# A hybrid SSD / RWKV-7 layer with a ConvGLU on one core: other plans for the recurrence phase, steps cut in two, and the SSD step sizes half a chunk sooner

## The chip, the core and the metric

The kernel runs on one core of a Trainium2 chip. The metric is the device time of one execution in microseconds (us); the time of a kernel is the median of its runs. The engines are named as the profile names them: PE (TensorE, matmuls; PEld its weight loads), DVE (VectorE), ACT (ScalarE), POOL (GpSimd) and SP (SyncE, which issues nearly all DMAs, in order). Each engine works its instructions off in program order.

## What is computed

The reference, cut to its skeleton (one layer, 2048 tokens, width 1024):

```python
xn = _rms_norm(h, pre_mix_norm[l])
proj = (xn @ w_in[l]).astype(jnp.float32)
p_ssd, p_rwkv = jnp.split(proj, [SSD_COLS], axis=-1)
y_ssd = _ssd_mixer(p_ssd, ...)      # conv, softplus step sizes, chunks of 128, gate, norm
y_rwkv = _rwkv7_mixer(p_rwkv, ...)  # token shift, low-rank decay and gates, 8 heads of 64
mix = jnp.concatenate([y_ssd, y_rwkv], axis=-1).astype(h.dtype) @ w_out[l]
h = h + _rms_norm(mix, post_mix_norm[l])
hn = _rms_norm(h, pre_ffn_norm[l])
u = _causal_dwconv(hn @ ffn_w_up[l], ffn_conv_w[l], ffn_conv_b[l])
gate, val = jnp.split(u, 2, axis=-1)
f = (jax.nn.silu(gate) * val) @ ffn_w_down[l]
h = h + _rms_norm(f, post_ffn_norm[l])
```

The RWKV-7 mixer is a recurrence over tokens, `S = S * w + sa * b + v * k` with `sa = S a`. The kernel computes it in chunks of 64 tokens, for which a triangular system per head and chunk has to be solved.

## The kernel before

Three phases follow one another, each a Python generator that emits instructions.

**Recurrence phase** (`phase_R`): 16 blocks of 128 tokens. A block normalises and transposes its tokens (`load`), multiplies them with 14 column groups of `w_in` (steps `d.0` to `d.13`, two per PSUM bank, 24 matmuls each) and with 8 groups for the SSD convolution (`conv.0` to `conv.7`, 24 matmuls each, followed by six tap instructions per pair of groups on DVE and two on POOL). From the `d` results come the decay (`low_rank`: tanh, two small matrix products `zw` and `za` in 16 matmuls, a running sum), the keys (`keys`, `norm`, `receptance`), the Gram matrices (`gram`, chunks 0 and 1) and the triangular solve: `solve` writes blocks of the Gram matrix to DRAM (`ATd`), reads them back laid out one system per partition (`atl`), runs 31 steps of two small tensor instructions each (`tmp`, then `xl`; 62 instructions, each needing the one before), and sends the result through DRAM (`XTd`) into `XT`. The block before (`b`) uses its `XT`: `own`, `merge` (`XW` on DVE, `pw` and `po` on PE), `update`, `state`, `gate`, and `finish` (group norm, transposes `yt`, output).

What is emitted in which order is a written plan: one string per kind of iteration (`FIRST`, `SECOND`, `PLAN` for blocks 2 to 14, `LAST`, and `DRAIN`, in which `S` runs a step of the SSD phase). `f` is the block of this iteration, `b` the block before, `n` the next one. PE runs exactly the order of the plan. On the other engines a scheduler orders the instructions and keeps dependencies; each of them is in order at run time too, so an instruction that waits holds everything behind it on its engine.

**SSD phase** (`phase_S`): 16 chunks of 128 tokens, in pairs. `steps` computes the step sizes of a pair (32 short matmuls `dt` and some 20 instructions of 128x16 on DVE, up to `da`), `sums` the running sums (matmul `acs`), `flip` and `rows` bring them into rows; then decay, state, output projection (`o`), `post` (norm, residual, transposes `ht`). `S_PLAN` is the order within a chunk; `s.` steps run in even chunks, `t.` steps in odd ones, both for the next pair.

**Feed-forward phase** (`phase_F`): up and down products of the ConvGLU, a seven-product scheme on halves.

The lines that matter below: L193 and L197 (`load`), L206 (the matmuls of `d` and `conv`), L384, L388, L389, L394 (`low_rank`: the low part of the operand `WX`, the two kinds of matmul, the running sum), L367 (taps), L443 and L447 (Gram and its masked copy `G`), L459, L463, L477, L483 (the DMAs of `solve`), L471 and L474 (its steps), L515 (`XW`), L522 (`pw`), L611 to L617 (`finish` up to `yt`), L790 and L795 (`da`, `acs`), L978 and L983 (`xi`, `ht`).

## Time and profile before

| | us |
|---|---|
| three runs | 2787.14, 2790.0, 2790.8; median 2790.0 |
| the profiled execution | 2795.42, of which its span is 2793.4 |
| recurrence phase with its drain | 0 to about 1069 (last `yt`) |
| SSD phase | to about 1470 |
| feed-forward phase | the rest |

In the stretch from 140 to 960 us, blocks 2 to 14 and a little more, PE is busy for 745.7 of 820 us, DVE for 617.4, ACT for 422.8 and POOL for 336.2, and the mean granted TensorE clock is 0.96. From 1130 to 1400 us, in the SSD phase, PE is busy for 244.5 of 270 us.

How to read the rows that follow: a row of the timeline has the start, the duration, the engine, the line, the operation, the tiles, the count, and in brackets how long the engine sat idle before it and what ended that. A row of the waits has the waiting instruction, what released it, the total in us, the number of times and the longest. A row of the windows has the busy time (with the number of instructions) of PE, PEld, DVE, ACT and POOL, then the granted clock of TensorE, the share of the DMA engines and GB/s. The chain of waits is followed back from the last instruction; "issue" in it is time for which the profile shows no wait. Matmul groups with "xN" are N matmuls in a row.

### The profile page before, as it was taken

The page shows a single profiled execution, that of the slowest core. Times are in us where ns is not written, and L with a number is a line of the kernel's source. Part 1 is how long each engine was busy: PE and PEld are TensorE (multiplying, and loading weights), DVE is VectorE, ACT ScalarE, POOL GpSimd, SP SyncE. Part 2 cuts the span into 40 slices and gives each one's busy share as a digit, 9 for nine tenths or more (in the row PEclk, how much of TensorE's full clock was granted, in tenths as well). Part 3 has the DMA queues.
Part 4 walks back from the last instruction along what each step waited for, and adds up shares of the span by engine and source line. Part 5 has one row for each costly group of instructions (what it writes and reads, how often), then busy time and mean ns, then how long its engine had stood idle before and what let it go on. Part 6 is the DMA issues. An engine that isn't in the chain of part 4 may idle for free.

```text
span 2793.4 us, 54157 instructions
## 1 busy us (share of the span) xinstructions
PE 2533.3 (91%) x21458; PEld 1595.1 (57%) x21468; DVE 1942.4 (70%) x3711; ACT 1196.6 (43%) x2448; POOL 1237.7 (44%) x1286
## 2 busy tenths in 40 slices
PE   5898899999989989899898798989988899999998
PEld 5888888888878865455443343434433344444443
DVE  7778767777777766556767858787879744554557
ACT  5455555445555534344444444434344333132132
POOL 5234434434434423333457855657476532132234
PEclk8999999999999989999999899999999999999999
DMA  6212121221211144333355334343434633333243
GB/s 213 52 43 60 47 48 45 52 51 43 60 47 45 40 149 137 107 105 124 136 183 190 126 138 155 136 154 132 151 129 155 226 99 106 102 101 102 86 137 126
DMA packets 261278, 302.62 MB, mean 108 GB/s; under 512 B 133664, under 2 KB 168864, under 8 KB 257696
## 3 DMA queue, kind: packets, MB, share of 16 engines
q1 hardware_dynamic: 259440, 296.54, 33.4%
q8 instruction: 168, 2.75, 0.4%
q10 hardware_dynamic: 1584, 2.63, 0.3%
q14 instruction: 86, 0.70, 0.1%
HBM read 188.11 MB, written 110.99 MB: 107 GB/s over the span
## 4 chain that ended last, share of the span: by engine, by line
PE 42%; DVE 25%; POOL 11%; DMA 8%; issue 8%; ACT 4%; SPq 2%; POOLq 0%; DVEq 0%; ACTq 0%
PE u L1182 16%; PE d L1329 10%; PE d L206 4%; DVE ca L367 3%; PE o L958 3%; DVE xl L474 3%; DVE tmp L471 3%; POOL fa L1087 2%; DMA HN<-hT 2%; DMA atl<-ATd 2%; DVE a L1219 2%; POOL us L1083 1%; PE l L1410 1%; POOL p L1247 1%; DMA ATd<-G 1%
## 5 line engine op out<-in xcount | busy, mean ns | idle before, releaser
L1182 PE MATMUL u<-b,w 128*128 128x512 f16 x3696 | 820.4, 384 | 52.1 <-DVE C L1191 36.5
L1182 PEld LDWEIGHTS <-w 128*128 128x128 f16 x3696 | 365.3, 99 | 503.5 <-issue 80.5
L206 PE MATMUL d<-xt,wr 128*128 128x129 f16 x5376 | 356.3, 230 | 7.2 <-DVE xt L197 5.1
L206 PEld LDWEIGHTS <-wr 128*128 128x128 f16 x5376 | 346.0, 103 | 28.9 <-issue 23.0
L1329 PE MATMUL d<-dw,fa 128*128 128x512 f16 x1512 | 339.8, 384 | 18.3 <-DVE dw L159 17.6
L1329 PEld LDWEIGHTS <-fa 128*128 128x128 f16 x1596 | 158.1, 99 | 222.7 <-issue 34.7
L1191 DVE TENSOR_TENSOR C<-u,C 128x512 f32<-128x512 f32 x220 | 150.6, 685 | 188.6 <-PE u L1182 151.4
L206 PE MATMUL c<-xt,wc 128*128 128x131 f16 x3072 | 201.2, 223 | 0.3 <-ACT tr L344 0.3
L206 PEld LDWEIGHTS <-wc 128*128 128x128 f16 x3072 | 184.7, 98 | 5.8 <-issue 0.7
L367 DVE SCALAR_TENSOR_TENSOR ca<-rc,cw,ca 128x128 f32<-128x128 f32 x384 | 156.5, 440 | 39.9 <-POOL ca L362 38.3
L1338 DVE TENSOR_TENSOR acc<-d,acc 128x512 f32<-128x512 f32 x212 | 139.8, 682 | 57.3 <-PE d L1329 56.6
L1219 DVE SCALAR_TENSOR_TENSOR p<-C,fpar,p 128x1024 f32<-128x1024 f32 x88 | 121.8, 1384 | 70.2 <-ACT p L1217 70.1
L159 DVE SCALAR_TENSOR_TENSOR w<-us,w 128x512 f16<-128x512 f32 x132 | 121.4, 925 | 68.2 <-ACT w L158 67.1
L471 DVE TENSOR_TENSOR tmp<-atl,xl 128x60 f32<-128x60 f32 (+24 forms) x496 | 122.1, 246 | 52.2 <-DMA atl<-ATd 41.9
L1086 ACT ACTIVATE fa<-p 128x512 f16<-128x512 f32 x132 | 79.6, 624 | 177.4 <-DVE p L1223 94.1
L1087 POOL TENSOR_TENSOR fa<-p,fa 128x512 f16<-128x512 f32 x120 | 151.5, 1273 | 3.6 <-ACT fa L1086 3.6
L474 DVE TENSOR_TENSOR xl<-xl,tmp 128x60 f32<-128x60 f32 (+24 forms) x496 | 137.4, 277 | 11.8
L158 ACT ACTIVATE w<-us 128x512 f16<-128x512 f32 x132 | 80.5, 623 | 139.3 <-POOL us L1083 99.9
L1219 DVE SCALAR_TENSOR_TENSOR a<-C,fpar,a 128x1024 f32<-128x1024 f32 x88 | 128.9, 1465 | 4.5 <-ACT a L1217 1.7
L362 POOL TENSOR_SCALAR ca<-rc,cw,cb 128x128 f32<-128x128 f32 x128 | 69.7, 553 | 135.4 <-ACT rc L359 61.7
L1216 POOL COPY C<-fcarry 128x2 f32<-128x2 f32 x88 | 40.9, 467 | 158.4 <-ACT a L1217 77.3
L1221 POOL COPY fcarry<-C 128x2 f32<-128x2 f32 x88 | 34.4, 391 | 169.1 <-DVE C L1191 168.7
(318 smaller groups left out, 4583.9 us busy)
## 6 DMA issues: line engine op xcount, KB each, us to landing
UW<-w SPq DMA_DIRECT2D x154, 256.0 KB
w<-UW SPq DMA_DIRECT2D x154, 256.0 KB
us<-in_w_u_dram SPq DMA_DIRECT2D x44, 512.0 KB
DW<-dw SPq DMA_DIRECT2D x70, 256.0 KB
dw<-DW SPq DMA_DIRECT2D x56, 256.0 KB
hs<-HN SPq DMA_DIRECT2D x48, 256.0 KB
r<-in_w_d_dram SPq DMA_DIRECT2D x10, 1024.0 KB
xin<-in_x_dram SPq DMA_DIRECT2D x16, 512.0 KB
```

Of the source, the lines that this page charges most:

```text
L159: eng.scalar_tensor_tensor(out=lo, in0=src, scalar=scale, in1=hi, op0=ALU.mult, op1=ALU.subtract)
L206: nc.tensor.matmul(ps, w[:, a, kt, :], xt[:, kt, b, cols], start=n == 0, stop=n == 3 * KT - 1)
L367: V.scalar_tensor_tensor(out=acc[:, q], in0=raw[:, q, k:k + 128], scalar=cw[:, g + q, k:k + 1], in1=acc[:, q], op0=ALU.mult, op1=ALU.add)
L471: V.tensor_tensor(out=tmp[:, :m, :n], in0=atl[:, j, j + 1:32].unsqueeze(1).to_broadcast([P, m, n]), in1=xl[:, :m, j:j + 1].to_broadcast([P ...
L474: V.tensor_tensor(out=xl[:, :m, j + 1:32], in0=xl[:, :m, j + 1:32], in1=tmp[:, :m, :n], op=ALU.add)
L958: nc.tensor.matmul(self.po, l, WO[:, v, (kt + 4) % KT, ds_], start=k == 0, stop=k == 23)
L1087: eng.tensor_tensor(out=lo, in0=src, in1=hi, op=ALU.subtract)
L1182: nc.tensor.matmul(bk[at], self.w[i][:, u, k, :], self.half.b[i][:, k, v, :], start=start and n == 0, stop=n == 11, skip_group_check=True)
L1191: V.tensor_tensor(out=o, in0=ps, in1=a, op=ALU.add)
L1219: V.scalar_tensor_tensor(out=a, in0=c[:, 2 - d:1026 - d], scalar=cw[:, g, 2 - d:3 - d], in1=a, op0=ALU.mult, op1=ALU.add)
L1329: nc.tensor.matmul(ps, pairs[m].a[i][:, u, t * P:t * P + P], ws[n][m][:, v, :], start=new and m == 0 and u == v == 0, stop=m == N - 1 and ...
L1338: V.tensor_tensor(out=acc[j][:, t], in0=ps, in1=acc[j][:, t], op=ALU.add)
```

## The change

Every plan of the recurrence phase is rewritten; of the tables a line or two is shown, and what they do to the engines further down. `low_rank` becomes `low.0` (tanh and operand split) and `low.1` (matmuls and running sum), `finish` becomes `finish.0` (the statistics, at the end of an iteration) and `finish.1` (transposes and output, emitted in the iteration after, as `a.finish.1`), `load` becomes `load.0` and `load.1` with work between them.

```diff
 S_PLAN = """
-c.begin c.decay.0 Z c.off p.norm c.keys Z c.decay.1 p.o.0.0 Z t.sums p.o.0.1 t.flip Z n.rows q.post.0 c.y c.state
-p.o.1.0 q.post.1 p.o.1.1 s.steps
+c.begin c.decay.0 Z c.off p.norm c.keys Z c.decay.1 p.o.0.0 Z t.sums s.steps p.o.0.1 t.flip Z n.rows q.post.0 c.y c.state
+p.o.1.0 q.post.1 p.o.1.1
...
 PLAN = """
-f.d.0 f.d.1 b.values f.d.2 f.d.3 f.low_rank f.d.4 f.d.5 f.keys f.d.6 ...
+f.d.0 f.d.1 f.d.2 a.finish.1 b.values f.d.3 f.low.0 f.d.4 f.d.5 f.low.1 f.d.6 f.d.7 f.d.8 f.keys f.d.9 f.conv.0
...
-            def low_rank(self):
+            def low(self, part):
+                sides = [(slice(64 * i, 64 * i + 64), slice(64 - 64 * i, 128 - 64 * i)) for i in range(2)]
+                if part == 0:
+                    X = self.X = wk.tile([P, 2, P], F16, name="WX" + self.sf, tag="WX")
+                    S.activation(WA[0:64], WA[0:64], AF.Tanh)
+                    for i, (own, far) in enumerate(sides):
+                        S.activation(X[own, i], WA[own], AF.Copy)
+                        V.tensor_tensor(out=X[far, i], in0=WA[own], in1=X[own, i], op=ALU.subtract)
+                    S.activation(GL, GL, AF.Tanh, scale=0.5)
+                    V.tensor_scalar(out=GL, in0=GL, scalar1=0.5, scalar2=0.5, op0=ALU.mult, op1=ALU.add)
+                    return
...
                     for j in range(4):
                         js = slice(j * P, (j + 1) * P)
-                        nc.tensor.matmul(ps[:, j, :], wl[:, i, js], X[:, i], start=True, stop=False)
-                        nc.tensor.matmul(ps[:, j, :], wl[own, 2, js], X[own, i], start=False, stop=True)
+                        nc.tensor.matmul(
+                            ps[:, j, :], wl[:, i, js], X[:, i], start=j == 0, stop=False, skip_group_check=True)
+                    for j in range(4):
+                        js = slice(j * P, (j + 1) * P)
+                        nc.tensor.matmul(
+                            ps[:, j, :], wl[own, 2, js], X[own, i], start=False, stop=j == 3, skip_group_check=True)
...
-                cum = self.tl("cum", tag="kkn")
+                cum = Pv
...
                 for q in range(4):
-                    nc.sync.dma_start(
+                    K.marks["atl"] = nc.sync.dma_start(
...
+                chain = G_ if it == iters - 1 else V
                 for j in range(31):
                     n, m = 31 - j, j // 4 + 1
-                    V.tensor_tensor(
+                    chain.tensor_tensor(
...
-            nc.sync.dma_start(st, w_z[g])
+            pace(tc, K, nc.sync.dma_start(st, w_z[g]), "atl")
...
-            nc.sync.dma_start(self.xt, XN[self.b])
+            pace(tc, K, nc.sync.dma_start(self.xt, XN[self.b]), "atl")
...
-            nc.sync.dma_start(self.xbc, XC[self.b])
+            pace(tc, K, nc.sync.dma_start(self.xbc, XC[self.b]), "atl")
```

So: the running sum is written where `Pv` will stand and no longer into the buffer of `kkn`; the 62 solve instructions of the last block go to POOL instead of DVE; and the first loads of the SSD phase stand behind the `atl` reads on SP's queue (`pace` adds an order to the queue, no wait). Lines of the changed kernel are shifted by up to 22.

**The matmuls of the low-rank step on PE**, in block 6. Before, these rows follow the last matmul of `d.3` and go on alternating, a matmul of 128 rows (L388) and one of 64 (L389), eight times for `zw` and `za` together:

```order
L206 MATMUL d_2_7707<-xt_7455,wr 128x129
L388 LDWEIGHTS wl
L388 MATMUL zw_7768<-WX_7765,wl 128x128
L389 LDWEIGHTS wl
L389 MATMUL zw_7768<-WX_7765,wl 128x128
```

Now they follow the last matmul of `d.5`; this is the place, after four matmuls of 128 rows (L404), where the four of 64 rows (L408) begin:

```order
L404 LDWEIGHTS wl
L404 MATMUL zw_6753<-WX_6690,wl 128x128
L408 LDWEIGHTS wl
L408 MATMUL zw_6753<-WX_6690,wl 128x128
L408 LDWEIGHTS wl
```

The step has moved 48 matmuls (`d.4` and `d.5`) back, `yt`, `vt` and `bo` now stand between `d.2` and `d.3`, and the two shapes change four times in a block instead of sixteen.

**DVE, from the arrival of `XT` to the Gram matrix**, in block 6. Before, from the transposes `XW` to the last masked copy `G` of the first chunk (`kkn`, `AR`, `BK` are the normalised keys and the Gram operands, `tr` and `tk` receptance and key, `ca` taps):

```order
L515 STREAM_TRANSPOSE XW_7011<-XT_232 32x256 x2
L415 SCALAR_TENSOR_TENSOR kkn_6565<-sq_6564,kkn_6565 128x512
L346 SCALAR_TENSOR_TENSOR tr_6563<-raw_8_6936,mus,tr_6563 128x128
L423 SCALAR_TENSOR_TENSOR AR_6571<-kkn_6565,Pi_6570 128x4x128
L346 SCALAR_TENSOR_TENSOR tr_6563<-raw_8_6936,mus,tr_6563 128x128
L434 TENSOR_TENSOR AR_6571<-tr_6563,Pi_6570 128x4x2x64
L427 SCALAR_TENSOR_TENSOR BK_6572<-tha_6567,sq_6564 128x4x128
L436 SCALAR_TENSOR_TENSOR tr_6563<-tr_6563,par,tk_6562 128x128 x4
L367 SCALAR_TENSOR_TENSOR ca_0_6998<-rc_0_6996,cw,ca_0_6998 128x128 x5
L447 TENSOR_TENSOR G_6575<-gr_6_7058,cst 128x512
L367 SCALAR_TENSOR_TENSOR ca_0_6998<-rc_0_6996,cw,ca_0_6998 128x128
L447 TENSOR_TENSOR G_6575<-gr_6_7059,cst 128x512
```

Now, from the second `XW`:

```order
L536 STREAM_TRANSPOSE XW_6984<-XT_232 32x256
L440 TENSOR_TENSOR tk_6540<-tk_6540,tm_7006 128x512
L357 SCALAR_TENSOR_TENSOR tr_6541<-raw_8_6891,mus,tr_6541 128x128 x2
L454 TENSOR_TENSOR AR_6549<-tr_6541,Pi_6548 128x4x2x64
L456 SCALAR_TENSOR_TENSOR tr_6541<-tr_6541,par,tk_6540 128x128 x4
L378 SCALAR_TENSOR_TENSOR ca_0_6971<-rc_0_6969,cw,ca_0_6971 128x128 x6
L435 SCALAR_TENSOR_TENSOR kkn_6543<-sq_6542,kkn_6543 128x512
L383 SCALAR_TENSOR_TENSOR ca_0_6971<-ct_0_6980,ca_0_6971 128x256
L443 SCALAR_TENSOR_TENSOR AR_6549<-kkn_6543,Pi_6548 128x4x128
L447 SCALAR_TENSOR_TENSOR BK_6550<-tha_6545,sq_6542 128x4x128
L378 SCALAR_TENSOR_TENSOR ca_2_7091<-rc_2_7089,cw,ca_2_7091 128x128 x6
L467 TENSOR_TENSOR G_6553<-gr_6_7144,cst 128x512
```

The receptance and the first taps have moved ahead of `kkn`, the product `tk` has come in, and all taps of two convolution pairs stand ahead of the first `G`. Behind this place, the token load (L193 and L197 before), the running sum (L394) and the second pair of `tk` have moved out of the 62 solve instructions: 33 other instructions stood among those in block 6 before, 23 do now.

**DVE, the step sizes of the SSD phase**, for the fourth pair. Before, they stand in the odd chunk, from `dv` to `da`, mixed with that chunk's work; this is the end of them (L796 reads the result of `acs`, which needs `da`):

```order
L786 SCALAR_TENSOR_TENSOR dq_19098<-dq_19098,de_19097 128x16
L787 SCALAR_TENSOR_TENSOR dq_19098<-dq_19098,ds_19099 128x16
L887 TENSOR_TENSOR Xd_19193<-Xdt_19125,dec_19128 128x512
L789 SCALAR_TENSOR_TENSOR dtt_19100<-dq_19098,dv_19096 128x16
L790 TENSOR_TENSOR da_19101<-dtt_19100,Ab 128x16
L796 TENSOR_SCALAR nac_19102<-acs_19219 128x16
L978 SCALAR_TENSOR_TENSOR xi_18939<-m_18941,pnr,gpre_18185 128x1024
```

Now they follow `xi` of the even chunk, and `da` is done 12 rows ahead of L812, which reads `acs`:

```order
L947 TENSOR_TENSOR ST_17283<-pst_19070,ST_17283 128x512
L803 SCALAR_TENSOR_TENSOR dq_18985<-dq_18985,ds_18986 128x16
L805 SCALAR_TENSOR_TENSOR dtt_18987<-dq_18985,dv_18983 128x16
L806 TENSOR_TENSOR da_18988<-dtt_18987,Ab 128x16
L935 TENSOR_SCALAR yt_18862<-yt_18862,sgr 128x256 x2
L865 TENSOR_TENSOR Xdt_19109<-px_19113,dtt_18518 128x512
```

The whole chain has moved from the first half of the odd chunk into the second half of the even one. The order of the feed-forward phase's own lines is the same on every engine.

More of the change, by code (lines that the diff above doesn't have):

```diff
@@ L113 @@
 """
 SECOND = """
[L115 to L117 removed]
+f.d.0 f.d.1 f.d.2 b.values f.d.3 f.d.4 f.d.5 f.low.0 f.low.1 f.d.6 f.conv.0 f.d.7 f.keys b.own.0 f.d.8 f.d.9 f.conv.1
+f.norm f.conv.2 f.conv.3 f.receptance f.conv.4 b.merge.0 f.gram.0 b.merge.1 f.conv.5 f.gram.1 b.update.0 n.load.0
@@ new lines @@
+b.state.0 b.own.1 n.load.1 f.conv.6 f.conv.7 b.update.1 f.d.10 f.d.11 f.solve f.d.12 b.state.1 f.transposed.0
+f.transposed.1 b.gate f.d.13 b.finish.0
+"""
+PLAN = """
+f.d.0 f.d.1 f.d.2 a.finish.1 b.values f.d.3 f.low.0 f.d.4 f.d.5 f.low.1 f.d.6 f.d.7 f.d.8 f.keys f.d.9 f.conv.0
+b.own.0 f.conv.1 b.merge.0 f.norm f.conv.2 b.merge.1 f.conv.3 f.conv.4 b.update.0 f.receptance f.gram.0 f.conv.5
+f.gram.1 n.load.0 b.state.0 n.load.1 f.conv.6 b.own.1 f.conv.7 b.update.1 f.d.10 f.solve f.d.11 f.d.12 f.transposed.0
@@ L127 @@
+b.own.1 S S b.update.1 S b.state.1 b.gate S b.finish.0 b.finish.1
 """
@@ L175, in rsqrt_cols, with norm_rows @@
     return r
-def norm_T(tc, K, work, psp, pstag, src, g, dst, col, sfx, between=None, junk=None):
+def norm_rows(tc, K, work, src, sfx, junk):
     nc = tc.nc
@@ L635, in phase_R @@
         blocks = [Block(it) for it in range(iters)]
-        blocks[0].load(None)
+        blocks[0].load(0)
+        blocks[0].load(1)
         for g in range(14):
```

106 lines of the change are left out of this document (47 added, 59 removed).

## The prediction

> **What bounds the kernel now.** The first view is the page's table of engines: PE is the busiest, so a change must shorten PE's work or its waits. The second is PE's waits in blocks 2 to 14; then the chain of waits, for what sets the length of a block.
>
> ```profile
> PE 2533.3 (91%) x21458; PEld 1595.1 (57%) x21468; DVE 1942.4 (70%) x3711; ACT 1196.6 (43%) x2448; POOL 1237.7 (44%) x1286
> ...
> PE zw L388 <- DVE WX L384: 26.2, 14, 2.7
> PE yt L617 <- POOL ysb L613: 18.0, 13, 1.4
> PE pS L585 <- ACT UV L568: 12.4, 13, 1.7
> PE gr L443 <- DVE BK L427: 8.6, 13, 0.7
> PE pt L191 <- DVE xin L193: 7.9, 12, 0.7
> ```
>
> The five waits are 73.1 us of 820. In the chain one row returns once per block:
>
> ```profile
> 176.54 1.26 issue
> 235.48 1.26 issue
> 971.58 1.26 issue
> ```
>
> From the first to the last are 13 blocks, (971.58 - 176.54)/13 = 61.16 us each; 820 us hold 13.4 blocks, so 73.1 us are 5.45 us of waiting per block. The first block alone took 58.94. What the others have more stands in the granted clock (the column behind POOL's) around one `zw` wait:
>
> ```profile
> 464.00:472.00 8.00, 8.00 (x69) 6.52 (x69) 4.93 (x20) 2.39 (x9) 3.23 (x5) 0.57 0.14 33
> ...
> 463.65 0.23 PE L388 MATMUL zw<-WX,wl 128*128 128x128 f16 x1 [1.81 <-DVE WX L384]
> 466.87 9.12 PE L206 MATMUL d<-xt,wr 128*128 128x129 f16 x120
> ...
> 528.41 7.07 PE L206 MATMUL d<-xt,wr 128*128 128x129 f16 x120
> ```
>
> PE waits 1.81 us for `WX`, then for 8 us it is busy throughout at a mean clock of 0.57: 8 x 0.43 = 3.4 us lost, and the 120 matmuls behind take 9.12 us instead of 7.07. On average over the 13 blocks this is 61.16 - 58.94 = 2.2 us. So a block is 53.5 us of PE work at full clock, 5.45 of waits and 2.2 of slow clock. (The Trainium skill, "TensorE: Matmul & The Clock Gate", "Part 1: The HAM clock gate", lets the clock fall after an idle window of about 3.4 us; by that rule a wait of 1.81 us costs no clock, and the sum below would be 13 x 2.2 = 29 us less gain. The rows show the fall, and decide.)
>
> Beside PE stands a second loop, through the solve. DVE is in order, and `XW`, which waits for `XT`, stands ahead of the Gram operands of the next block:
>
> ```profile
> 418.56 0.43 DVE L515 STREAM_TRANSPOSE XW<-XT 32x256 f32<-32x256 f32 x1 [0.69 <-DMA XT<-XTd]
> 440.41 0.19 DVE L471 TENSOR_TENSOR tmp<-atl,xl 128x31 f32<-128x31 f32 x1 [1.64 <-DMA atl<-ATd]
> 473.09 0.17 DVE L474 TENSOR_TENSOR xl<-xl,tmp 128x8 f32<-128x8 f32 x1
> 480.28 0.43 DVE L515 STREAM_TRANSPOSE XW<-XT 32x256 f32<-32x256 f32 x1 [3.16 <-DMA XT<-XTd]
> ...
> 433.23 0.60 DVE G L447
> ```
>
> From `XW` to the last `G` 15.3 us (418.56 to 433.83), through `ATd` and `atl` 6.6 (to 440.41), the solve 32.85 (to 473.26), through `XTd` and `XT` 7.0 (to 480.28): 61.7 us, the block. PE and this loop are equally long, and the solve holds much that isn't solve: 62 instructions at the 0.17 to 0.19 us of its first and last are 11.
>
> **The change, recurrence phase.** *PE work.* The low-rank matmuls alternate between 128 and 64 rows:
>
> ```profile
> 956.69 0.23 PE L389 MATMUL zw<-WX,wl 64*128 64x128 f16 x1
> ...
> 959.10 8.68 PE L206 MATMUL d<-xt,wr 128*128 128x129 f16 x120
> ```
>
> The first row is the second of the sixteen, so 15 take 2.41 us (956.69 to 959.10), 0.16 each and 2.57 together, against 7.07/120 = 0.059 for matmuls of one shape. With 4 changes of shape instead of 16: 16 x 0.059 + 4 x 0.10 = 1.34, that is 1.2 us less per block (bounds: nothing, or all of 2.57 - 0.94 = 1.6). PE's floor is 53.5 - 1.2 = 52.3.
>
> *The `zw` wait.* `d.4` and `d.5`, 48 matmuls or 2.8 us, now lie between the operand and its use, so the 1.81 us go, and with them the slow clock, if no wait as long takes their place.
>
> *The `yt` wait.* In front of `yt` lies a chain over four engines:
>
> ```profile
> 442.52 1.14 PE L593 MATMUL pq<-UV,G 64*64 64x64 f32 x16
> 443.59 0.66 PE L493 MATMUL bt<-cst,BK 128*128 128x128 f32 x4
> 448.60 1.06 PE L601 MATMUL zg<-GL,g 128*128 128x128 f32 x8
> 453.86 0.66 PE L617 MATMUL yt<-cst,ysb 128*128 128x128 f32 x4 [1.44 <-POOL ysb L613]
> ...
> 444.81 0.62 ACT L610 ACTIVATE y<-ysb 128x512 f32<-128x512 f32 x1
> ...
> 448.63 0.68 DVE L611 TENSOR_REDUCE vr<-y 128x8 f32<-128x512 f32 x1
> ```
>
> From the end of `pq` on PE (443.66) to `yt` (453.86) are 10.2 us, of which 3.2 are `vr` standing behind other work on DVE (445.43, where `y` ends, to 448.63). So it is 7.0 us at least. In the new order PE has `zg`, `bt` and 96 matmuls of `d` in between: 1.06 + 0.66 + 96 x 0.059 = 7.4. What remains is `vr`'s delay on DVE, 0 to 3.2; the order puts it behind 15 of the 31 solve steps, and I take 1.0.
>
> *The other waits.* `BK` has a PE distance like before (0.67 per block, kept). The second Gram matrix gets a new wait, since six taps stand ahead of `G`, whose reading frees its bank: six at 0.3 (the `tk` row below has two such operations of 128 elements in 0.61) against 24 x 0.059 = 1.4 us of matmuls between; with the mask itself, 0.60 in the `G` row, 0.1 to 1.5, taken 0.7. `pt`, 0.66 before, stays. `pS` goes. `pw` behind `XW` waits by what the loop is late, 0 to 2: 0.2. Together 1.0 + 0.67 + 0.7 + 0.66 + 0.2 = 3.2, none as long as 1.81, so PE's block would be 52.3 + 3.2 = 55.5.
>
> *The solve loop.* Ten instructions leave the solve: four halves of the token load (512 elements each, 0.6 as in the `G` row), two taps (0.3 each), the running sum, and the second pair of `tk` with its wait on ACT:
>
> ```profile
> 468.09 1.22 DVE L394 TENSOR_TENSOR_SCAN cum<-cst,thw 128x512 f32<-128x512 f32 x1
> 472.56 0.61 DVE L346 SCALAR_TENSOR_TENSOR tk<-raw,mus,tk 128x128 f32<-128x128 f32 x2 [3.19 <-ACT tk L344]
> ```
>
> 2.4 + 0.6 + 1.2 + 0.6 + 3.2 = 8.0, the solve is 24.85. The load falls into the 6.6 us of DMA, in which DVE waited anyway. From `XW` to `G` a product `tk` of 512 elements comes in, 15.9 us. Loop: 15.9 + 6.6 + 24.85 + 7.0 = 54.35. On SP one `YR` write now stands between the `XTd` and `XT` issues, where the queue waits for `XTd` to land anyway: nothing. PE's 55.5 is the longer one. I take **55.5 us** per block; the ends are the floor, 52.3, and a block whose new waits add up to the old, 58.9.
>
> 13 x (61.16 - 55.5) = 73.6 us (29 to 115).
>
> *Blocks 0 and 1* (to 176 us) get the new PE work and lose a `zw` wait each, but wait for weights too: 6 us (0 to 14).
>
> **The drain.** Before, the last `atl` read sits behind SSD weight loads on SP:
>
> ```profile
> 428.87 1.16 PE L443 MATMUL gr<-AR,BK 64*128 64x128 f32 x16
> 981.22 1.75 PE L443 MATMUL gr<-AR,BK 64*128 64x128 f32 x16 [0.74 <-DVE G L447]
> ...
> 986.19 3.25 SPq L724 DMA_DIRECT2D sst<-in_w_z_dram  x2
> ...
> 998.47 0.19 DVE L471 TENSOR_TENSOR tmp<-atl,xl 128x31 f32<-128x31 f32 x1 [4.75 <-DMA atl<-ATd]
> 1029.96 0.17 DVE L474 TENSOR_TENSOR xl<-xl,tmp 128x8 f32<-128x8 f32 x1
> ...
> 1040.95 0.24 PE L522 MATMUL pw<-XW,G 32*32 32x32 f32 x2 [4.92 <-DVE XW L515]
> ...
> 456.19 1.26 POOL L622 TENSOR_TENSOR yln<-yln,tv 128x512 f32<-128x512 f32 x1 [2.39 <-ACT yln L620]
> ...
> L1381 POOL TENSOR_TENSOR fs<-fss 128x1 f32<-128x1 f32 x16 | 7.8, 493 | 5.4 <-ACT fj L1378 5.2
> ```
>
> From the end of the last Gram matmul to the first solve step are 15.5 us (982.97 to 998.47), in block 6 10.4 (430.03 to 440.41); SP's queue gives 3.25 of them to two weight loads. `pace` is worth 5. Then the solve took 31.7 us on DVE (to 1030.13). No row shows such a step on POOL. Its nearest, `fs`, takes 0.49 us for one element; POOL's operations of 512 elements take about twice DVE's (1.26 against 0.60 to 0.68), so by ratio the small step is 2 x 0.17 = 0.34. I take 0.4: 62 steps are 25 us (0.19, as on DVE, to 0.49: 12 to 30). POOL's own work among them, two `tS`, three pairs of taps, a group norm and four products, ten operations at 1.2, is 12: 37 (24 to 42). So 5 won, 5 lost: 0, from 13 gained to 6 lost. What covers a longer solve is SSD work on PE; `pw` waited 4.92 us with the old one, and each us more is lost in full. (The Trainium skill, "GPSIMD Engine Reference", "3.1 Elementwise", has POOL's two-input operation 1.96 times as long as DVE's; estimated from that page a step is 0.21 x 1.96 = 0.41 us, and the sum the same.)
>
> **SSD phase.** `acs` waits for `da` once per pair:
>
> ```profile
> PE acs L795 <- DVE da L790: 20.8, 6, 4.8
> ...
> 1208.74 0.65 PE L983 MATMUL ht<-ident_s,xi 128*128 128x128 f32 x4 [1.68 <-DVE xi L978]
> ...
> 1230.00:1240.00 10.00, 8.02 (x41) 5.04 (x42) 5.24 (x13) 1.97 (x5) 2.07 (x3) 0.83 0.02 7
> ```
>
> Six waits, 20.8 us, and behind each a slow clock (in the window behind one of them 0.83 over 10 us: 1.7 us, 10 in all). With `dt` and `da` half a chunk sooner, 12 us of the 25 that a chunk takes (401 us for 16), all this goes, 31. But odd chunks then meet the wait for `xi` that even chunks show (1.68 at 1208.74): 6 x 1.5 = 9; and the 20 small DVE instructions, some 0.2 us each, now stand ahead of `yt` in the even chunk: 4 per pair, of which I let one pair in six pay. Net 18 (8 to 28). The cover is the PE work of `o`, `ht`, `py`; without it `acs` would wait as before. The feed-forward phase keeps its order: nothing.
>
> **Sum.** 73.6 + 6 + 0 + 18 = 97.6 us. The profiled execution is 2795.42, 5.4 above the median; from the median, 2790.0 - 97.6 = **2692**.
>
> **Rivals.**
> *The solve loop stays the bound, or a wait of some 2 us at `pw` keeps the slow clock:* for it speaks that PE and the loop differ by 1 us and that PE's old `zw` wait was already DVE's fault. A block of 58.9: 13 x 2.3 + 6 + 18 = 54, **2736**.
> *The waits only move:* `vr` is as late as before, `yt` waits 3.2 and takes the slow clock (3.4) over: 52.3 + 0.67 + 0.7 + 0.66 + 3.2 + 3.4 = 60.9; 13 x 0.2 + 6 + 18 = 27, **2763**.
> *Slower: POOL stretches the solve.* A two-input step on DVE that meets a two-input operation of POOL ends with it, here with the one of 456.19 quoted above, which ends at 457.45:
>
> ```profile
> 456.31 1.24 DVE L471 TENSOR_TENSOR tmp<-atl,xl 128x75 f32<-128x75 f32 x1
> ```
>
> 1.24 us instead of some 0.2. (The Trainium skill, "GPSIMD Engine Reference", "1. Specifications", has the SBUF interfaces shared between the two engines; the rows agree.) In the new order ten POOL operations of a block run during the solve. If each stops a step for 1.05 us on top of what it has now, the solve is 35 and the loop 64.8: 13 x 3.6 - 24 = 23 lost, **2813**. It decides from a loop of 63 us on, a solve of 33.4. Against it: four or five of the ten already stand in the old solve, and 61.7 contains them.
>
> **How the numbers follow.** Forecast 0.57; loop bound 0.20; waits moved 0.10; stretched solve 0.07; gains and losses that cancel within 0.2% (5.6 us, about what a measurement of this kernel can tell from no change) 0.06. The range, 2650 to 2768, takes in block lengths from 52.7 to 60.9 with the bounds of drain and SSD phase; it leaves out the last two cases (0.13) and some 0.05 below. Faster 0.87, same 0.06, slower 0.07.
>
> **What would show it.** Right: the period of `XW` near 55.5, PE's clock 1.00 through blocks 2 to 14, no `zw` row among PE's waits, no `acs` row, `z` matmuls between `dt` and `acs`. The low-rank step: 16 starts in about 1.3 us. Wrong: a `pw` or `yt` wait above 1.8 us followed by a clock of 0.5; solve steps of over 1 us in number; in the drain a `pw` wait well over 4.9 us.

## The result: 2726 us, and the profile after

The changed kernel takes 2725.96 us (median of 4 runs, 2723.75 to 2729.76) against 2790.4 for the kernel before on the same chip: a ratio of 0.9762, interval 0.9744 to 0.9779, some 64 to 66 us less. The forecast was 2692, the range 2650 to 2768. The two profiled executions differ by 71.4 us (spans 2793.4 and 2722.0). Cut at four places that both have, the difference divides like this:

| part | before | after | change | forecast |
|---|---|---|---|---|
| to the third block's `XW` | 235.1 | 223.8 | -11.3 | -6 (blocks 0 and 1) |
| the next 12 blocks | 735.8 (61.31 each) | 688.9 (57.40 each) | -46.9 | -68 (55.5 each) |
| from there to `acs` of the second pair (end of the recurrence, drain) | 110.2 | 118.6 | +8.5 | -6 (one block more, and a drain of 0) |
| from there to the first `u` matmul (SSD phase) | 369.6 | 344.2 | -25.4 | -18 |
| feed-forward phase | 1342.8 | 1346.5 | +3.7 | 0 |

The last row is not counted as an effect of the change: in the profiles of all fourteen kernels of this study, whose feed-forward phase is the same, this part took 1339 to 1347 us.

The row of the engines on the page after:

```profile
PE 2500.4 (92%) x21468; PEld 1580.4 (58%) x21468; DVE 1951.3 (72%) x3649; ACT 1209.6 (44%) x2448; POOL 1251.6 (46%) x1348
```

PE is the busiest engine as before, with 33 us less of busy time. The ends of the 12 blocks in DVE's timeline, in the kernel before and then in the changed one:

```profile
235.06 0.43 DVE L515 STREAM_TRANSPOSE XW<-XT 32x256 f32<-32x256 f32 x1 [2.26 <-DMA XT<-XTd]
...
970.83 0.44 DVE L515 STREAM_TRANSPOSE XW<-XT 32x256 f32<-32x256 f32 x1 [1.93 <-DMA XT<-XTd]
```

```profile
223.80 0.43 DVE L536 STREAM_TRANSPOSE XW<-XT 32x256 f32<-32x256 f32 x1 [2.33 <-DMA XT<-XTd]
...
912.66 0.44 DVE L536 STREAM_TRANSPOSE XW<-XT 32x256 f32<-32x256 f32 x1 [1.14 <-DMA XT<-XTd]
```

A block takes (970.83 - 235.06)/12 = 61.31 us before and (912.66 - 223.80)/12 = 57.40 us after. PE's waits after in these blocks:

```profile
PE pt L201 <- DVE xin L203: 28.4, 12, 2.4
PE gr L463 <- DVE BK L447: 9.3, 11, 1.2
```

The `zw`, `yt` and `pS` waits are gone. In their place `pt` waits 2.4 us in every block, where the forecast had 0.66. One such place in PE's timeline:

```profile
531.80 1.08 PE L201 MATMUL pt<-cst,xin 128*128 128x128 f32 x4 [2.37 <-DVE xin L203]
532.68 2.80 PE L216 MATMUL c<-xt,wc 128*128 128x131 f16 x24
...
537.48 1.57 PE L216 MATMUL c<-xt,wc 128*128 128x131 f16 x24
...
559.73 0.39 PE L404 MATMUL zw<-WX,wl 128*128 128x128 f16 x4
...
561.03 5.18 PE L216 MATMUL d<-xt,wr 128*128 128x129 f16 x87
```

and the window behind the wait (the granted clock stands behind POOL's busy time):

```profile
531.80:535.80 4.00, 4.00 (x40) 3.78 (x42) 3.73 (x7) 1.70 (x3) 1.35 (x3) 0.57 0.56 139
```

After the wait of 2.37 us the clock is 0.57 for 4 us, 1.7 us lost, and 24 matmuls take 2.80 us instead of 1.57. The last two rows of the timeline are the grouped low-rank step: sixteen matmuls from 559.73 to 561.03, 1.30 us, as forecast (1.34).

With (1 - clock) x length summed over the windows of the 12 blocks, and the waits summed, a block can be divided into work, waits and slow clock:

| per block, us | work at full clock | waits | slow clock | sum |
|---|---|---|---|---|
| before | 53.34 | 5.45 | 2.52 | 61.31 |
| forecast | 52.3 | 3.2 | 0 | 55.5 |
| after | 52.42 | 3.25 | 1.73 | 57.40 |

Work and waits came out as forecast, though the waits are other ones. The slow clock, which the forecast had going away with `zw`, stayed for the most part.

Each row of this table is one execution. Two kernels further down have the same order in these blocks as the changed one (`a_nopace`, `a_drainV`): 57.52 and 57.88 us per block, with 1.88 and 2.18 of slow clock. `b_newS` has the blocks of before: 60.94, with 1.89. So a difference of up to 0.5 us per block, or 0.6 of slow clock, between two profiles shows nothing.

Beside PE stands the loop through the solve. Its legs, from `XW` to `XW`, add up to the block in any case; that it holds the block is a matter for the experiments. In the timeline, DVE's rows of one block first, then two of POOL:

```profile
512.08 0.44 DVE L536 STREAM_TRANSPOSE XW<-XT 32x256 f32<-32x256 f32 x1 [3.06 <-DMA XT<-XTd]
...
513.75 1.65 DVE L357 SCALAR_TENSOR_TENSOR tr<-raw,mus,tr 128x128 f32<-128x128 f32 x2
...
517.44 1.90 DVE L378 SCALAR_TENSOR_TENSOR ca<-rc,cw,ca 128x128 f32<-128x128 f32 x6
...
522.84 1.91 DVE L378 SCALAR_TENSOR_TENSOR ca<-rc,cw,ca 128x128 f32<-128x128 f32 x6 [0.28 <-POOL ca L373]
...
526.77 2.66 DVE L378 SCALAR_TENSOR_TENSOR ca<-rc,cw,ca 128x128 f32<-128x128 f32 x3 [0.49 <-POOL ca L373]
529.35 1.28 DVE L467 TENSOR_TENSOR G<-gr,cst 128x512 f32<-128x512 f32 x2
...
536.96 0.19 DVE L492 TENSOR_TENSOR tmp<-atl,xl 128x31 f32<-128x31 f32 x1 [1.35 <-DMA atl<-ATd]
...
562.47 0.17 DVE L495 TENSOR_TENSOR xl<-xl,tmp 128x8 f32<-128x8 f32 x1
...
568.73 0.44 DVE L536 STREAM_TRANSPOSE XW<-XT 32x256 f32<-32x256 f32 x1 [1.60 <-DMA XT<-XTd]
...
514.00 1.27 POOL L449 TENSOR_TENSOR BK<-tk,Pv 128x512 f32<-128x512 f32 x1 [3.04 <-ACT qs L579]
...
527.25 2.03 POOL L511 TENSOR_TENSOR BK<-BK,Pi 128x1024 f32<-128x1024 f32 x1
```

`XW` to the last `G` takes 18.6 us here (512.08 to 530.63), through `ATd` and `atl` 6.3, the solve 25.7 (to 562.64), and 6.1 to the next `XW`. As means of the 12 blocks:

| leg of the loop, us | before | forecast | after |
|---|---|---|---|
| `XW` to the last `G` | 15.7 | 15.9 | 18.8 |
| through `ATd`, `atl` | 7.2 | 6.6 | 6.6 |
| solve | 32.2 | 24.85 | 25.3 |
| through `XTd`, `XT` | 6.3 | 7.0 | 6.7 |
| sum (of the unrounded legs) | 61.3 | 54.35 | 57.4 |

Three legs are within 0.5 us of the forecast. In the first, fifteen taps and two products `ca<-ct,ca` stand ahead of the last `G` where eleven and one stood, some 1.6 us more. And POOL stretches DVE: the pair of `tr` at 513.75 takes 1.65 us instead of 0.6 beside the product of 514.00, which before had run ahead of `XW`; three taps at 526.77 take 2.66 beside that of 527.25, as such taps did before (undisturbed, six take 1.90, at 517.44).

### The profile page after: what moved, and what is told of

It reads as the page before. It is cut to its first block, busy times and chain, and to the rows that moved or that the text cites. A ratio compares the mean times of both kernels' runs of the same rounds, so it can differ in the third digit from the quotient of the medians.

```text
span 2722.0 us, 54074 instructions
## 1 busy us (share of the span) xinstructions
PE 2500.4 (92%) x21468; PEld 1580.4 (58%) x21468; DVE 1951.3 (72%) x3649; ACT 1209.6 (44%) x2448; POOL 1251.6 (46%) x1348
## 4 chain that ended last, share of the span: by engine, by line
PE 40%; DVE 26%; POOL 13%; DMA 8%; issue 6%; ACT 4%; SPq 2%; POOLq 0%; DVEq 0%; ACTq 0%
PE u L1198 16%; PE d L1345 9%; PE d L216 3%; DVE ca L378 3%; DVE xl L495 3%; DMA HN<-hT 2%; PE c L216 2%; DVE tmp L492 2%; POOL fa L1103 2%; POOL us L1099 2%; DVE a L1235 2%; PE o L974 2%; PE l L1426 1%; POOL p L1263 1%; DMA XTd<-xl 1%
## 5 line engine op out<-in xcount | busy, mean ns | idle before, releaser
L216 PE MATMUL d<-xt,wr 128*128 128x129 f16 x5376 | 325.7, 221 | 5.3 <-DVE xt L207 3.4
L216 PEld LDWEIGHTS <-wr 128*128 128x128 f16 x5376 | 315.8, 98 | 17.6 <-issue 13.3
L216 PE MATMUL c<-xt,wc 128*128 128x131 f16 x3072 | 218.9, 233 | 8.7 <-ACT wc L291 4.6
L216 PEld LDWEIGHTS <-wc 128*128 128x128 f16 x3072 | 206.0, 104 | 22.3 <-issue 8.2
L378 DVE SCALAR_TENSOR_TENSOR ca<-rc,cw,ca 128x128 f32<-128x128 f32 x384 | 147.2, 417 | 35.0 <-POOL ca L373 32.0
L495 DVE TENSOR_TENSOR xl<-xl,tmp 128x60 f32<-128x60 f32 (+24 forms) x465 | 137.2, 295 | 12.5
L373 POOL TENSOR_SCALAR ca<-rc,cw,cb 128x128 f32<-128x128 f32 x128 | 82.9, 656 | 117.0 <-ACT rc L370 94.0
```

The costliest lines, as they stand in the source:

```text
L216: nc.tensor.matmul(ps, w[:, a, kt, :], xt[:, kt, b, cols], start=n == 0, stop=n == 3 * KT - 1)
L373: G_.tensor_scalar(out=acc[:, q], in0=raw[:, q, 3:131], scalar1=cw[:, g + q, 3:4], scalar2=cb[:, g + q:g + q + 1], op0=ALU.mult, op1=ALU.add)
L378: V.scalar_tensor_tensor(out=acc[:, q], in0=raw[:, q, k:k + 128], scalar=cw[:, g + q, k:k + 1], in1=acc[:, q], op0=ALU.mult, op1=ALU.add)
L495: chain.tensor_tensor(out=xl[:, :m, j + 1:32], in0=xl[:, :m, j + 1:32], in1=tmp[:, :m, :n], op=ALU.add)
```

## The experiments

Four questions were open: whether PE or the loop holds the block, what the parts are worth alone, where the slow clock comes from, and what the drain lost. The three sets of four kernels ran on three chips, on which the kernel before took 2790.7, 2797.2 and 2788.6 us, so ratios are compared; the changed kernel has 0.9762.

### The low-rank grouping alone, and taken back

Kernel before with the grouped matmuls; and the changed kernel with the alternating ones:

```diff
-                        nc.tensor.matmul(ps[:, j, :], wl[:, i, js], X[:, i], start=True, stop=False)
-                        nc.tensor.matmul(ps[:, j, :], wl[own, 2, js], X[own, i], start=False, stop=True)
+                        nc.tensor.matmul(
+                            ps[:, j, :], wl[:, i, js], X[:, i], start=j == 0, stop=False, skip_group_check=True)
+                    for j in range(4):
+                        js = slice(j * P, (j + 1) * P)
+                        nc.tensor.matmul(
+                            ps[:, j, :], wl[own, 2, js], X[own, i], start=False, stop=j == 3, skip_group_check=True)
```

> The kernel before with the sixteen low-rank matmuls of a block grouped by shape, every engine's order else unchanged. Theory A (the block of before was held by the DVE loop through XW, Gram, solve and XT, 61 us, and PE was only as long because it waited): the matmuls take 1.2 us less per block, the wait ahead of zw or pS grows by the same, and the time moves by 0 to -6 us, to 2784 to 2791. Theory B (PE was the bound and each us of its work counts): 16 blocks by 1.2 us, -19 us, 2771.

2763.4 us, ratio 0.9898 (0.9873 to 0.9923), 28 us less: more than either theory said. Theory A falls, and B's price is too low. The block is 58.93 us, 2.4 less, of which only 0.9 is work. Its waits in these blocks, and one low-rank step in PE's timeline:

```profile
PE zw L388 <- DVE WX L384: 21.9, 12, 1.8
```
```profile
451.84 0.40 PE L388 MATMUL zw<-WX,wl 128*128 128x128 f16 x4 [1.83 <-DVE WX L384]
452.17 0.39 PE L392 MATMUL zw<-WX,wl 64*128 64x128 f16 x4
452.50 0.40 PE L388 MATMUL za<-WX,wl 128*128 128x128 f16 x4
452.83 0.60 PE L392 MATMUL za<-WX,wl 64*128 64x128 f16 x4
453.37 8.37 PE L206 MATMUL d<-xt,wr 128*128 128x129 f16 x120
```

The `zw` wait is still there, 1.83 us here and 21.9 in the 12 blocks (21.7 before). But the sixteen matmuls behind it take 1.5 us (451.84 to 453.37) instead of 3.2 (463.65 to 466.87 in the rows of the prediction), and the slow clock falls from 2.52 to 0.88 us per block. So most of the slow clock had come neither from the wait alone nor from the alternating matmuls alone, in which PE starts a matmul only every 0.16 to 0.22 us, but from the two together. Over the kernels of this study the trace counts as follows, with 24 blocks (two kernels of 12) in each row; in these blocks half speed always comes in stretches of 3.4 or 6.8 us, which lose 1.7 or 3.4:

| low-rank step | kernels | starts with half speed within 3.4 us | of these 6.8 us long |
|---|---|---|---|
| wait of 1.8 us, alternating | `before`, `b_newS` | 21 of 24 | 9 |
| wait of 1.8 us, grouped | `b_lowgrp`, `b_grp_newS` | 9 of 24 | 0 |
| no wait, alternating | `a_lowalt`, `a_plans` | 0 of 24 | 0 |

Why the two together count for so much more than either isn't shown.

> The changed kernel with the alternating low-rank matmuls of before, every engine's order else unchanged. Theory A (the DVE loop of 57.5 us sets the block and PE waits 3.3 us in each): 1.2 us more PE work per block is taken from the waits of pt for xin; 0 to +5 us, 2726 to 2731. Theory B (PE sets the block): 16 blocks by 1.2 us, +19 us, 2745.

2736.8 us, ratio 0.9807 (0.9786 to 0.9829): 13 us more by the ratios than the changed kernel, between the two theories. PE's waits in the 12 blocks:

```profile
PE pt L201 <- DVE xin L203: 28.3, 12, 2.4
PE gr L459 <- DVE BK L443: 0.7, 2, 0.4
```

Work rises by 1.2 us per block (to 53.58) and the `gr` wait for `BK` falls from 9.3 us to 0.7 in 12 blocks; the block is 57.76, only 0.36 longer, which is no more than profiles of one order differ by. In the steady blocks theory A holds: PE has slack against the loop. Of the 13.7 us by which the spans differ, 4.3 come from the 12 blocks, 4.9 had come before them (the third block's `XW` at 228.7 instead of 223.8) and the rest behind them. None of this can be put down to the alternating matmuls from one profile: `a_plans`, which has the same order up to there on PE, DVE, ACT and POOL, has this `XW` at 222.3. The ratios do differ beyond their intervals; where the 13 us arise stays open.

### The SSD order alone, and both parts together

The second kernel has the new `S_PLAN` in the kernel before, the third also the grouped matmuls:

```diff
-c.begin c.decay.0 Z c.off p.norm c.keys Z c.decay.1 p.o.0.0 Z t.sums p.o.0.1 t.flip Z n.rows q.post.0 c.y c.state
-p.o.1.0 q.post.1 p.o.1.1 s.steps
+c.begin c.decay.0 Z c.off p.norm c.keys Z c.decay.1 p.o.0.0 Z t.sums s.steps p.o.0.1 t.flip Z n.rows q.post.0 c.y c.state
+p.o.1.0 q.post.1 p.o.1.1
```

> The kernel before with the new order of the SSD chunk alone. Theory A (the SSD gain is independent of the recurrence phase): six pairs by 3.7 us, some 22 us, and up to 25 with the last pair: 2765 to 2769; no wait of acs for da, some ten waits of ht for xi. Theory B (part of what the changed kernel gains there comes from the other state in which it leaves the drain): 10 us or less, 2780 or more.

2768.3 us, ratio 0.9919 (0.9898 to 0.9940), 23 us less, theory A. PE's waits of the phase hold no `acs` row for `da`; `ht` waits eleven times:

```profile
PE ht L983 <- DVE xi L978: 12.1, 11, 1.7
```

> The kernel before with two parts of the change, the grouped low-rank matmuls (alone -27 us) and the new SSD chunk order (alone -22 us), and the old plans. Theory A (the two add up, and the rewritten plans, the drain and the pacing are worth only what is left of the change, some 15 us): -49 us, 2739 to 2743. Theory B (the two share a gain, or the plans carry most of the change): 2750 or more.

2736.55 us, ratio 0.9791 (0.9770 to 0.9812), 58 us less (52 to 64) where 28 and 23 make 51: theory A, the two don't share a gain. The whole change is 0.9762, so all the rest of it (plans, drain, `pace`) brings about 0.3% beside these two, 8 us, but the two intervals overlap.

### The plans alone

Both parts taken back in the changed kernel (the two diffs above, reversed).

> The changed kernel with the alternating low-rank matmuls and the SSD order of before: the new plans with the drain's changes alone. The two parts taken back gave 27 and 22 us by themselves in the kernel before. Theory A (the plans and the grouping end the same slow clock, so each is worth more alone than beside the other): the plans alone are worth 25 to 40 us, 2750 to 2765, ratio 0.986 to 0.991. Theory B (the plans are worth the 8 us by which the whole change beats the two parts): 2778 to 2786, ratio 0.995 to 0.999.

2755.5 us, ratio 0.9869 (0.9836 to 0.9902), 37 us less than before: theory A. Alone the plans (with the drain and `pace`) bring 37 us, the grouping 28, the SSD order 23; that is 88, and together they bring 66. Plans and grouping take the same slow clock away, that behind `zw`: the plans put 48 matmuls in front of the alternating step, so that no wait precedes it, the grouping shortens it. The division of the block shows it. Grouping alone lowers the slow clock by 1.64 us per block; beside the plans it leaves it where it is, 1.74 without and 1.73 with it, all behind `pt`. And the 1.3 us of PE work that it saves beside the plans (53.72 to 52.42) return in part as waits (2.40 to 3.25), of which `gr` for `BK` is the new one.

### What holds the block

Three edits of the changed kernel, and two pairs of them. PE's order changes only where the edit says so; on DVE, ACT and SP the scheduler moves some rows with each. The second half of the token load one step later:

```diff
-f.gram.1 n.load.0 b.state.0 n.load.1 f.conv.6 b.own.1 f.conv.7
+f.gram.1 n.load.0 b.state.0 f.conv.6 n.load.1 b.own.1 f.conv.7
```

> The changed kernel with the second half of the token load one step later in the plan of blocks 2 to 14, so that the 24 matmuls of conv.6 run in front of its transposes pt, which waited 2.4 us per block for xin. Theory A (the DVE loop of XW, Gram, solve and XT sets the block at 57.4 us and PE's waits are slack): the wait of pt goes, another takes its place, the block stays within 0.5 us, 2720 to 2728. Theory B (PE sets the block and the wait with its slow clock is on the path): 1.4 us of wait and some 1.3 us of slow clock less per block, -30 to -38 us, 2690 to 2697.

2720.9 us, ratio 0.9729 (0.9711 to 0.9747), and a block of 57.5 us. PE's waits in its 12 blocks:

```profile
PE pw L543 <- DVE XW L536: 13.9, 18, 1.7
...
PE pt L201 <- DVE xin L203: 12.2, 12, 1.2
```

Theory A: the `pt` wait is more than halved, the slow clock falls from 1.73 to 1.16 us per block, and the block doesn't move; PE now waits for `XW`, which is the loop. (DVE's order changed too, but the loop's legs only trade 0.7 us: 19.6 from `XW` to `G`, 24.7 in the solve.) The 0.3% it gained (or did not, the intervals touch) didn't come from these blocks.

POOL's product of `BK` and `Pi` on ACT:

```diff
-                    G_.tensor_tensor(out=BK8, in0=BK8, in1=self.Pi[:, :, 64:65].to_broadcast([P, 8, P]), op=ALU.mult)
+                    for n in range(8):
+                        S.activation(BK8[:, n], BK8[:, n], AF.Copy, scale=self.Pi[:, n, 64:65])
```

> The changed kernel with POOL's product of BK and Pi (2.03 us), which stretches two or three taps on DVE in front of the last Gram mask by 1.6 us per block, on ACT as eight small activations. Theory A (the loop sets the block and that stretch is a leg of it): the leg from XW to the last G falls from 18.6 to some 17.0 us, the block to 55.8 to 56.3, -13 to -20 us, 2706 to 2713. Theory B (PE sets the block, or ACT's eight activations delay UV and ysb by as much): within 5 us of 2726.

2719.9 us, ratio 0.9722 (0.9703 to 0.9741). The block is 57.28, a fall smaller than profiles of one order differ by, and not what theory A said. The stretch is gone from DVE's timeline, but not the time:

```profile
517.14 0.42 DVE L383 SCALAR_TENSOR_TENSOR ca<-ct,ca 128x256 f32<-128x256 f32 x1 [0.43 <-ACT ct L382]
518.70 1.00 DVE L378 SCALAR_TENSOR_TENSOR ca<-rc,cw,ca 128x128 f32<-128x128 f32 x3 [1.13 <-POOL ca L373]
```

Three taps take 1.00 us instead of 2.66, and DVE waits 1.13 us ahead of them, for the POOL tap that starts the accumulation. The leg from `XW` to `G` is 18.3 instead of 18.8, while the solve's grew by 0.3. A stretch that ends together with something else is worth only the difference.

The last ten solve steps left out in blocks 1 to 14, so that `XT` isn't the solution:

```diff
-                for j in range(31):
+                for j in range(31 if it in (0, iters - 1) else 21):
```

> The changed kernel with only the first 21 of 31 solve steps in blocks 1 to 14, the last ten being left out. Theory A (the loop sets the block): the solve leg is 5 us shorter, so PE becomes the bound: its work at full clock and small waits, 54 to 55.5 us per block, -26 to -44 us, 2682 to 2700, the pt wait unchanged or smaller. Theory B (PE sets the block): the block stays at 57 us, within 6 us of 2726.

2716.5 us, ratio 0.9718 (0.9698 to 0.9737). The solve's leg falls to 16 us, but the block only to 56.6: with `XW` early, the leg from `XW` to `G` grows to 27 us, 6.6 of them idle (1.3 in the changed kernel). Theory A fell short here, B said no change; the row of waits tells why:

```profile
PE pt L201 <- DVE xin L203: 28.5, 12, 2.4
```

PE still waits 2.4 us in each block and still loses clock behind it. So shortening the loop gives 0.8 us, then PE with that wait is the bound. That led to both edits at once:

> The changed kernel with both single edits together: the last ten solve steps of blocks 1 to 14 left out and the second half of the token load one step later. Alone, the first left the block at 56.6 us (the loop shorter, PE's pt wait of 2.4 us still there), the second at 57.5 us (the wait halved, the loop unchanged). Theory A (two bounds stand within 1 us of each other, the loop and PE with its wait and slow clock, and only both edits move the block): 53.5 to 55.5 us per block, -26 to -50 us against 2726, 2676 to 2700. Theory B (a third thing holds the block at 56 to 57 us): within 5 us of what the first edit gave, 2712 to 2722 by its ratio.

2697.4 us, ratio 0.9665 (0.9625 to 0.9706), a block of 55.7 us, 0.2 above what theory A allowed; the time is in its range. Slow clock is 0.14 us per block. One edit gave 0.8 us per block, the other nothing, both 1.7:

```profile
PE pt L201 <- DVE xin L203: 10.4, 12, 1.0
PE nq L432 <- ACT sq L425: 9.7, 9, 1.9
```

So two bounds stand within 1 us of each other, and a single cure meets the other one. What holds the block at 55.7, waits of `pt`, `nq` and `gr` of 0.6 to 0.9 us each, was not taken further.

The two edits that compute everything, together:

> The changed kernel with the token load's second half one step later and the product of BK and Pi on ACT: a version that computes everything. Theory A (two bounds): the pt wait goes and the loop is some 0.5 us shorter, as the ACT version's leg from XW to G showed, so the block is 56.5 to 57 us and the time 2712 to 2722, ratio 0.969 to 0.973. Theory B (their single gains of 3 to 4 thousandths add): 0.968 or less.

2709.9 us, ratio 0.9704 (0.9663 to 0.9744), a block of 56.48 us with a slow clock of 0.70. It beats the kernel before by 3%; beside the changed kernel it is 0.6% ahead, with intervals that just touch (0.9744). The time is below theory A's range and the ratio in it; theory B isn't excluded by the interval, but the blocks fit A.

### The drain

The last solve back on DVE:

```diff
-                chain = G_ if it == iters - 1 else V
+                chain = V
```

> The changed kernel with the last block's solve on DVE as before. Theory A (POOL's solve of 37.9 us against 31.7 on DVE is what the drain lost): -4 to -6 us, 2720 to 2722. Theory B (with the solve on DVE its steps stand between the weight splits and each split of 1.2 us delays them, so that POOL's place was worth as much as it cost): within 2 us of 2726, or above. pw's wait and the time from the first solve step to the last tell which.

2729.7 us, ratio 0.9786 (0.9760 to 0.9812): theory B. The rows are the first and the last solve step of the last block, on POOL in the changed kernel and on DVE here:

```profile
940.62 0.24 POOL L492 TENSOR_TENSOR tmp<-atl,xl 128x31 f32<-128x31 f32 x1 [2.55 <-DMA atl<-ATd]
...
978.30 0.22 POOL L495 TENSOR_TENSOR xl<-xl,tmp 128x8 f32<-128x8 f32 x1
```
```profile
947.11 0.19 DVE L492 TENSOR_TENSOR tmp<-atl,xl 128x31 f32<-128x31 f32 x1 [1.06 <-DMA atl<-ATd]
...
983.27 0.17 DVE L495 TENSOR_TENSOR xl<-xl,tmp 128x8 f32<-128x8 f32 x1
```

On POOL the solve takes 37.9 us, as forecast (37), on DVE 36.3, not the 31.7 of before: in the new order 23 taps and four weight splits stand among its steps. Where the solve runs makes no difference that can be measured.

The first SSD loads without the order behind `atl`:

```diff
-            pace(tc, K, nc.sync.dma_start(st, w_z[g]), "atl")
+            nc.sync.dma_start(st, w_z[g])
...
-            pace(tc, K, nc.sync.dma_start(self.xt, XN[self.b]), "atl")
+            nc.sync.dma_start(self.xt, XN[self.b])
...
-            pace(tc, K, nc.sync.dma_start(self.xbc, XC[self.b]), "atl")
+            nc.sync.dma_start(self.xbc, XC[self.b])
```

> The changed kernel without the order on the SP queue that puts the SSD phase's first loads behind the last atl read. Theory A (pace is worth the 5 us by which the last solve starts sooner): +3 to +6 us, 2729 to 2732. Theory B (what the solve wins, the z matmuls lose, which wait 3.9 us for their late weights): within 3 us of 2726.

2734.3 us, ratio 0.9791 (0.9755 to 0.9827): 8 us by either measure, though the intervals overlap. The solve starts 16 us later (its first step in POOL's timeline; 14.5 later counted from the last `XW` of the 12 blocks) and `pw` waits for it (PE's waits from 905 us on):

```profile
956.96 0.24 POOL L492 TENSOR_TENSOR tmp<-atl,xl 128x31 f32<-128x31 f32 x1 [1.19 <-DMA atl<-ATd]
```
```profile
PE pw L543 <- DVE XW L536: 12.0, 2, 11.1
```

Theory A by its mechanism, with a larger price, since in this order weights and loads stand on SP's queue ahead of half of `ATd` as well as of `atl`. So neither POOL nor `pace` made the drain longer. What is new in it stands in the changed kernel's timeline, PE's rows first, then DVE's:

```profile
963.53 1.87 PE L846 MATMUL z<-ws,xs 128*128 128x512 f16 x4 [3.85 <-DVE ws L167]
...
990.99 1.06 PE L547 MATMUL po<-XT,XW 32*32 32x32 f32 x32 [2.89 <-ACT XW L553]
...
1018.26 1.12 PE L640 MATMUL yt<-cst,ysb 128*128 128x128 f32 x4 [7.32 <-POOL ysb L635]
...
1011.16 1.23 DVE L167 SCALAR_TENSOR_TENSOR wo<-ost,wo 128x1024 f16<-128x1024 f32 x1 [1.37 <-ACT wo L166]
...
1014.25 0.67 DVE L633 TENSOR_REDUCE vr<-y 128x8 f32<-128x512 f32 x1
```

`yt` of the last block waits 7.32 us, against 1.69 before, for a chain that begins with `vr` on DVE at 1014.25. `vr` stands behind the split of an output weight that waits for ACT and its load (1011.16). The plan before had five SSD steps between `gate` and `finish`; the new one has one, and none between the two parts of `finish`. `z` waits 3.85 us for weights that `pace` made later, and `po` 2.89. Against that `pw`'s old 4.92 is gone. Counted from the last `XW` of the 12 blocks, the drain runs like this:

| us after that `XW` | before | after |
|---|---|---|
| end of the last Gram matmul | 12.1 | 18.0 |
| first solve step | 27.6 | 28.0 |
| end of the solve | 59.3 | 65.9 |
| last `XW` | 69.6 | 72.2 |
| last `yt` | 97.7 | 105.6 |
| `acs` of the second pair | 110.2 | 118.6 |

So `pace` took 5.6 us out of the way from the Gram matrix to the solve, but the Gram matrix itself ends 5.9 us later, and the solve starts no sooner. Most of the loss, 5.3 of 8.5 us, arises between the last `XW` and `yt`. The granted clock is lower there too: over the whole stretch 0.88 in 118.6 us after, 0.92 in 110.2 before. That the waits make up the 8.5 us is read from the rows; the drain's plan was not tried by itself.

## Why the prediction was right, and where its terms were off

The time lies in the range and the direction was right; the gain was two thirds of what was forecast (66 of 97.6). The mechanism of the forecast, PE as the bound at full clock, is not what came. What came is the first rival, the loop as the bound and a wait that keeps the slow clock; it had a chance of 0.20 and 2736, and the 2726 measured lie nearer to that than to 2692. That the total isn't further off is partly luck: the SSD phase and blocks 0 and 1 brought 13 us more than forecast, while the drain lost.

- **PE's work** (53.5 to 52.3): right. 53.34 to 52.42, and sixteen low-rank starts in 1.30 us.
- **The waits** (3.2 in sum): right in sum, 3.25, wrong one by one. `yt` took 0 where 1.0 was put, the second Gram matrix 0.03 for 0.7, `BK` 0.78 for 0.67, and `pt` 2.37 for 0.66. For `pt` the prediction copied the old wait, though the rows of the new order on DVE show all taps of two pairs ahead of `G`, and `xin`, which `pt` waits for, stands behind these and `G`.
- **"None as long as 1.81, so no slow clock"**: this step failed. `pt` waits 2.37, and 1.73 us of slow clock stay per block. On PE's side 55.5 + 1.7 + 0.2 is 57.4. It isn't the only one: with the `pt` wait halved the block stayed at 57.5, because the loop was as long.
- **The `zw` wait as the cause of the slow clock**: half right at most. The grouping alone, with the wait unchanged, took away 1.64 of 2.52 us (1.0 against the 1.89 of `b_newS`, the smaller figure for the old blocks). (The Trainium skill, "TensorE: Matmul & The Clock Gate", "Part 1: The HAM clock gate", has the clock rise again only after a window of some 3.4 us in which PE was busy; half speed for one such window would be, as an estimate from that page, 1.7 us lost. The traces agree with that part: in these blocks 1.7 or 3.4 us are lost at a time, and 3.4 behind `zw` only where alternating matmuls follow it. That the clock falls only after an idle window of that length, they contradict: waits of 1.8 us were enough.)
- **The loop** (54.35, so that "PE's 55.5 is the longer one"): this step failed as well. The leg from `XW` to `G` takes 18.8 for 15.9, and the loop 57.4. The prediction added one product `tk` and missed four taps, a second `ca` product and the stretch of `tr` by a POOL product that has moved beside it. It also read the leg of before from the second of the two `XW` (418.56; the first is at 417.44), which made it 15.3 for a mean of 15.7. The solve (24.85, measured 25.3) and the DMA legs were right; by the rows of the trace nine instructions left the solve, from 32 to 23, not ten.
- **Rivals**: the first names what happened, but priced it at 58.9 us per block; it is 57.4, between it and the forecast, and the wait is at `pt`, not at `pw`. The waits did not move to `yt`. POOL stretches DVE in front of `G`, and in the solve as well, but little there: some 6 of the 62 steps of a block take over 0.5 us, some 4 before, and that adds about 1.0 us, where the rival had 10.
- **Blocks 0 and 1** (6): 11.3, of which the grouping alone gave 5.3 (its third block's `XW` is at 229.7). Two profiles of one order differ here by 6.4 us (`a_plans`, `a_lowalt`), so this isn't firm.
- **The drain** (0): 8.5 lost in a stretch that also holds the last block, for which 6 were to be gained. Both terms that were worked out came as said: the solve starts 9.9 us after the last Gram matrix instead of 15.5, and takes 37.9 us. But the Gram matrix ends 5.9 us later after `XW`, which is the first leg of the loop again, so the start wasn't earlier. Read from the rows, the rest of the loss lies in what was not looked at, the cover of `finish` and the time at which weights land.
- **The SSD phase** (18): 25.4. All `acs` waits went, as forecast. Six pairs take 47.05 us each instead of 50.71, by the rows of `acs` before and after; the last two rows are from PE's waits over just these six pairs, before and after:

```profile
1081.01 0.29 PE L795 MATMUL acs<-da,cst_s 128*128 128x16 f32 x2
...
1385.24 0.37 PE L795 MATMUL acs<-da,cst_s 128*128 128x16 f32 x2 [3.31 <-DVE da L790]
```
```profile
1031.30 0.29 PE L811 MATMUL acs<-da,cst_s 128*128 128x16 f32 x2
...
1313.57 0.39 PE L811 MATMUL acs<-da,cst_s 128*128 128x16 f32 x2
```
```profile
PE ht L983 <- DVE xi L978: 7.0, 5, 1.7
PE ht L999 <- DVE xi L994: 9.5, 8, 1.6
```

The 20.8 us of waits went, and so did the slow clock behind them (10.2 us over these pairs by the trace, 10 in the forecast). The mis-sized terms are the new ones: `ht` was to wait 9 us more, and waits 2.5 more; the delay of `yt`, put at 4, is 0.8.

## What to carry to other kernels

When a wait and a row of poorly filled matmuls stand together in front of a slow clock, test the matmuls alone: regrouping sixteen matmuls a block brought 28 us here with the wait untouched. When PE and a loop through other engines are equally long, forecast the change of both leg by leg, with every instruction that the new order puts ahead of a leg's end, and expect a single cure to be worth the distance to the other bound and no more. Parts that end the same loss don't add up: 28 and 37 us alone were some 43 together (66 less the 23 of the SSD order).
